# Neighbourhood attention scores as two 128-row matmuls, early loads issued later, and the last token tile normalized on VectorE

## The chip, the cores and the metric

The kernel runs on one core of a Trainium2 chip. The metric is the device time of one execution in microseconds (us), as the median of several runs. All times below are us unless ns is written.

## The reference

A two-layer encoder with model width 1024 runs over two sequences of 256 tokens (512 tokens in all). Layer 0 mixes with neighbourhood attention (8 heads of width 64 over a grid of 4 rows and 64 columns) beside a spatial gating unit; layer 1 mixes with latent attention beside a convolution. Each mixer and each convolutional feed-forward block is followed by a residual sum and a layernorm:

```python
def trunk(x, ...):
    for l in range(DEPTH):                      # DEPTH = 2
        m = even_mixer(...) if l % 2 == 0 else odd_mixer(...)
        x = layernorm(ALPHA * x + m, ln1_g[l], ln1_b[l])
        f = conv_ffn(x, ffn_w_up[l], ffn_conv_w[l], ffn_conv_b[l], ffn_w_down[l])
        x = layernorm(ALPHA * x + f, ln2_g[l], ln2_b[l])
    return x

def even_mixer(x, w_in, rpb, ...):
    h = x @ w_in                                # q, k, v, u, g
    a = neighbourhood_attention(q, k, v, rpb)   # softmax(q k^T / 8 + bias, masked) v
    b = spatial_gating(u, g, ...)
    return jnp.concatenate([a, b], axis=-1) @ w_out
```

## The kernel before

Everything is computed in 32-bit precision out of pairs of rounded numbers: a matrix X is held as hi(X), rounded to the matmul's number format, and lo(X) = X - hi(X). A product of two such matrices is three matmuls (hi hi, hi lo, lo hi). `wload` (L103 to L110) loads 128x1024 weights on SP's DMA queue, ScalarE (ACT) makes the hi part (L107) and VectorE (DVE) the lo part (L109); `split` (L112 to L114) does the same for activations.

The order of the work on each engine is set by a scheduler that simulates the program's timeline (`schedule_with_timeline_sim`, L881); each engine then runs its own list in order and waits on semaphores. `after_mm` (L98) makes an instruction wait for a given matmul: it paces loads.

`even_mixer` (L321) first computes the gating unit's inputs u and g over 8 slices k of the model width: per slice 256 KB of `xT` (tile `xraw`) and 512 KB of weights (`wug`, tile `raw`), both on SP's queue into a ring of four buffers, then 24 matmuls of 512 columns (tiles `u` and `dn`). Other early loads go by GpSimd's (POOL's) queue: parameters `par` (270 KB), the gating unit's layernorm rows `sgr` (512 KB), `sgb` (two of 256 KB), the attention `mask` (32 KB), and sixteen pieces of the attention bias (128 KB each, L388). All of them wait for the matmul `started`, the last of the first four. Fourteen of the sixteen bias pieces are issued ahead of the four small powers `rstd` (L162) of the gating unit's layernorm; POOL then adds the mask to the bias tiles (L392), multiplies and shifts the normalized values `vt` (L377, L378), and makes copies for the scores.

Then come v (`psv`), and, for each of four pairs of heads p, the projections of q (j = 0) and k (j = 1) (24 matmuls each, tile `qk`), written out of PSUM into the operands of the scores. Of the pair's two heads h, head 0 lies in partitions 0 to 63 and head 1 in 64 to 127. `qb` holds for head h hi(q) in the head's own 64 partitions and lo(q) in the other 64; `kh` holds hi(k) for both heads; `kb` holds lo(k) in the head's own partitions and hi(k), copied by POOL (L440), in the other 64. A score block of 128 queries and 256 keys is then

```python
            def score(out, h, qs, ks, qb=qb, kb=kb, kh=kh):
                mm(out, qb[near[h], h, qs], kh[near[h], ks], True, False)
                mm(out, qb[:, h, qs], kb[:, h, ks], False, True)
```

that is, one matmul over 64 partitions (hi hi) and one over 128 (hi lo + lo hi) into the same PSUM columns (tile `s`). There are 32 blocks: four pairs, two sequences, two query halves, two heads. Three sets of `qb` and `kb` serve the four pairs in turn; `kh` comes from another pool.

`attention` (L467) takes scores through DVE (scale and bias `er`, L452; row maximum `nmx`, L478), ACT (exponential, L481), DVE (reciprocal L484, scaling L489), TensorE (PE) transposes (tile `pt`, L494), an ACT copy (`PTr`, L496) and PE again (tile `pv`). Projections of later pairs, the gating unit's matmuls (`sg`) and the first part of the output projection (`op`, `dn`) stand between these in PE's list.

At the end of the kernel `ToOut.done` (L260) normalizes one token tile (128 tokens x 1024) after the other. After the residual sums (L197), the statistics (L258, L263) and POOL's power for the reciprocal deviation (L203), columns 0 to 831 (`ACUT`) are done by DVE in two passes (L268, L276) and leave on SP's queue (L278); columns 832 to 1023 are done by ACT (L271) and POOL (L272, L273) and leave on ACT's queue (L279). For the last tile (t = 3) DVE's second pass is cut in two pieces of 416 columns.

Of the kernel before, what the change touches and what calls it, by code (L numbers as in the profile page):

```python
# [8 lines left out]
F32 = mybir.dt.float32  # L9
F32R = mybir.dt.float32r  # L10
# [5 lines left out]
P = 128  # L16
D = 1024
# [28 lines left out]
def bcast_rows(ap, offset, n):  # L46
    return bass.AP(ap.tensor, offset, [[0, P], [1, n]])
# [3 lines left out]
def tile_encoder(ctx: ExitStack, tc: tile.TileContext, I, O):  # L51
# [23 lines left out]
    def small(w, s="s", tag="small", bufs=24):  # L75
        return sp.tile([P, w], F32, tag=tag, bufs=bufs, name=nm(s))
# [171 lines left out]
    class ToOut:  # L248
# [11 lines left out]
        def done(self, t):  # L260
            x = self.res.x[t]
            mv = small(2, "mv")
            nc.vector.bn_aggr(out=mv, in_=self.st[:, t])  # L263
            r = self.res.rstd(mv[:, 1:2], 1.0)
            a, b = slice(0, ACUT), slice(ACUT, 1024)
            nmr = small(2, "nmr")
            nc.vector.tensor_scalar(out=nmr[:, 0:1], in0=mv[:, 0:1], scalar1=-1.0, scalar2=None, op0=ALU.mult)  # L267
            nc.vector.scalar_tensor_tensor(out=x[:, a], in0=x[:, a], scalar=mv[:, 0:1], in1=self.rows[0][:, a],  # L268
                                           op0=ALU.subtract, op1=ALU.mult)
            nc.gpsimd.tensor_tensor(out=nmr[:, 1:2], in0=nmr[:, 0:1], in1=r, op=ALU.mult)  # L270
            nc.scalar.activation(out=x[:, b], in_=x[:, b], func=AF.Identity, scale=r, bias=nmr[:, 1:2])  # L271
            nc.gpsimd.tensor_tensor(out=x[:, b], in0=x[:, b], in1=self.rows[0][:, b], op=ALU.mult)  # L272
            nc.gpsimd.tensor_tensor(out=x[:, b], in0=x[:, b], in1=self.rows[1][:, b], op=ALU.add)  # L273
            cuts = (0, ACUT // 2, ACUT) if t == NT - 1 else (0, ACUT)
            for c0, c1 in zip(cuts, cuts[1:]):
                nc.vector.scalar_tensor_tensor(out=x[:, c0:c1], in0=x[:, c0:c1], scalar=r,  # L276
                                               in1=self.rows[1][:, c0:c1], op0=ALU.mult, op1=ALU.add)
                nc.sync.dma_start(out=self.y[t][:, c0:c1], in_=x[:, c0:c1])  # L278
            nc.scalar.dma_start(out=self.y[t][:, b], in_=x[:, b])  # L279

    class OutProj:
        def __init__(self, wname, mixT, g0, g1):
# [38 lines left out]
    def even_mixer():  # L321
        xT = []
        psu = [bank(pA, "u") for _ in range(4)]
        psg = dn_banks()
        started = None
        for k in range(KC):
            xr = rawp.tile([P, 1024], F32, tag="raw", name=nm("xraw"))
            x = act([P, 2, T], F32R, "xT")
# [1 line left out]
            if k == 0:  # L330
# [14 lines left out]
                for a, b in ((hi, 0), (hi, 1), (lo, 0)):  # L345
                    for c in range(4):
                        mm(psu[c], a[:, c * P:(c + 1) * P], x[:, b, :], a is hi and b == 0, False)
                    started = started or last_mm[0]
            else:
                nc.sync.dma_start(out=xr[:, :T], in_=I["xT"][k])  # L350
                split(x, xr[:, :T])
# [5 lines left out]
                    mm(psu[c], lo[:, sl], x[:, 0, :], False, k == KC - 1)  # L357
            for t in range(NT):
                gemm_tok([psg[t]], x, t, hi, lo, [slice(512, 1024)], k == 0, k == KC - 1)
        after_mm(nc.gpsimd.dma_start(out=par, in_=I["par"]), started)  # L360
        sgr = act([P, 1024], s="sgr")
        after_mm(nc.gpsimd.dma_start(out=sgr, in_=bcast_rows(I["sgu_rows"], 0, 1024)), started)
        sgb = act([P, 1024], s="sgb")
        after_mm(nc.gpsimd.dma_start(out=sgb[:, :512], in_=bcast_rows(I["sgu_rows"], 1024, 512)), started)
        after_mm(nc.gpsimd.dma_start(out=sgb[:, 512:], in_=I["sgu_wT"]), started)
# [48 lines left out]
        V = [act([P, 2, 512], s="V") for _ in range(2)]  # L414
        for t in range(NT):
            nc.scalar.copy(out=V[t // 2][:, t % 2, :], in_=psv[t])
        qks = [[act([P, 2, T], F32R, s="qk") for _ in range(2)] for _ in range(3)]
        for pair in qks:
            for q_ in pair:
                nc.gpsimd.memset(q_[:, 0, 0:1].bitcast(F32), 0.0)  # L420
        er, PTr = Ring(2, "er"), Ring(2, "PTr")
        for p in range(4):
            bias = biases[p]
            qb, kb = qks[p % 3]
            kh = tmp([P, T], F32R, s="kh")
            near = slice(0, 64), slice(64, 128)
            for j in range(2):
                ps = bank(pA, "qk")
                hi, lo = wload(I["wqk"][:, 2 * p + j].rearrange("p k n -> p (k n)"), 1024)
                gemm_feat(ps, hi, lo, xT)  # L430
                if j == 1:
                    nc.scalar.copy(out=kh, in_=ps)
                for h in range(2):
                    a, b = near[h], near[1 - h]
                    if j == 0:
                        nc.scalar.copy(out=qb[a, h, :], in_=ps[a])
                        nc.vector.tensor_tensor(out=qb[b, h, :], in0=ps[a], in1=qb[a, h, :].bitcast(F32),
                                                op=ALU.subtract)
                    else:
                        nc.gpsimd.tensor_copy(out=kb[b, h, :], in_=kh[a].bitcast(F32))  # L440
                        nc.vector.tensor_tensor(out=kb[a, h, :], in0=ps[a], in1=kh[a].bitcast(F32),
                                                op=ALU.subtract)

            def score(out, h, qs, ks, qb=qb, kb=kb, kh=kh):
                mm(out, qb[near[h], h, qs], kh[near[h], ks], True, False)
                mm(out, qb[:, h, qs], kb[:, h, ks], False, True)
            mixT[p] = act([P, 2, T], F32R, "mixT")

# [437 lines left out]
```

## Time and profile before

| | us |
|---|---|
| median of 3 runs (lowest, highest) | 1129.3 (1129.25, 1130.22) |
| the profiled execution's own time | 1130.04 |
| its span, first to last instruction | 1128.1 |
| PE busy in the span | 1100.6 (98%) |
| DVE busy | 664.6 (59%) |
| ACT busy | 491.0 (44%) |
| POOL busy | 231.6 (21%) |

Busy time of PE is modelled: a matmul is counted from its start to the end of its last column in the array, so consecutive matmuls overlap and a gap between their starts that is longer than usual need not show as idle time. The distance from one matmul's start to the next one's is read off the timeline. The 1.9 us by which the execution is longer than its span lie around the instructions.

### The profile page before, as it was taken

What the parts mean: (1) busy time and instruction counts of PE and PEld (TensorE: products, weight loads), DVE (VectorE), ACT (ScalarE), POOL (GpSimd) and SP (SyncE); (2) the same over time, 40 slices, a digit from 0 to 9 for tenths busy, and PEclk for the clock granted to TensorE, in tenths of its full rate; (3) what the DMA queues carried; (4) which work ended last, traced back from release to release, by engine and by line L of the source; (5) the groups of instructions that cost most, each with busy time, mean ns of one, the idle gap of its engine ahead of it and who ended that gap; (6) DMA issues with size and microseconds to landing.
All of it is one profiled execution on the core that took longest, in us unless ns stands there. A gap on an engine that the chain in (4) does not pass through costs nothing. (4 is left out here: it accounts for less than half of the span.)

```text
span 1128.1 us, 13661 instructions
## 1 busy us (share of the span) xinstructions
PE 1100.6 (98%) x5210; PEld 903.9 (80%) x5210; DVE 664.6 (59%) x996; ACT 491.0 (44%) x785; POOL 231.6 (21%) x231
## 2 busy tenths in 40 slices
PE   9999999999999999999998989999999999999995
PEld 7787767988888888888896767789888888888884
DVE  3567773686656565432369987567656566552226
ACT  3534552554444444321166779545444444431110
POOL 4081001300000000004456743521000000000264
PEclk9999999999999999999999989999999999999998
DMA  9742104343333333645232113135333333222601
GB/s 264 242 121 75 57 20 163 118 134 104 99 94 94 95 102 103 205 132 191 92 114 76 49 54 113 50 100 166 96 94 94 96 101 103 94 94 95 227 15 75
DMA packets 36193, 124.34 MB, mean 110 GB/s; under 512 B 4352, under 2 KB 5120, under 8 KB 36128
## 3 DMA queue, kind: packets, MB, share of 16 engines
q1 hardware_dynamic: 28224, 99.10, 28.8%
q0 software_dynamic: 6480, 22.66, 5.8%
q10 hardware_dynamic: 1424, 1.71, 0.6%
q8 instruction: 41, 0.67, 0.3%
q14 instruction: 24, 0.20, 0.1%
HBM read 114.01 MB, written 8.39 MB: 109 GB/s over the span
## 5 line engine op out<-in xcount | busy, mean ns | idle before, releaser
L96 PE MATMUL up<-xT,whi 128*128 128x512 f32 (+1 forms) x1536 | 440.5, 371 | 0.4 <-DVE xT L245 0.4
L109 DVE TENSOR_TENSOR wlo<-raw,whi 128x1024 fp32r<-128x1024 f32 (+1 forms) x174 | 223.2, 1284 | 303.3 <-ACT whi L107 297.0
L96 PEld LDWEIGHTS up<-xT,whi 128*128 128x128 f32 x1536 | 279.9, 188 | 50.6 <-DVE xT L245 0.6
L107 ACT CAST whi<-raw 128x1024 fp32r<-128x1024 f32 (+1 forms) x174 | 182.5, 1050 | 266.6 <-PE dn L96 132.4
L96 PE MATMUL up<-xT,wlo 128*128 128x512 f32 (+1 forms) x768 | 283.8, 372 | 0.0
L96 PE MATMUL dn<-whi,gT 128*128 128x512 f32 x704 | 217.5, 389 | 0.0
L96 PEld LDWEIGHTS up<-xT,wlo 128*128 128x128 f32 x768 | 144.3, 188 | 25.0
L96 PEld LDWEIGHTS dn<-whi,gT 128*128 128x128 f32 x704 | 132.0, 188 | 27.3
L96 PE MATMUL dn<-wlo,gT 128*128 128x512 f32 x352 | 136.9, 389 | 0.0
L182 POOL DMA_DIRECT2D xres<-xscr x12 | 6.5, 545 | 574.7 <-PE dn L96 573.9
L96 PEld LDWEIGHTS dn<-wlo,gT 128*128 128x128 f32 x352 | 66.1, 188 | 13.7
L113 ACT CAST gT<-cv 128x512 fp32r<-128x512 f32 x44 | 27.3, 620 | 111.9 <-DVE cv L747 111.9
L736 ACT ACTIVATE cv<-up,par 128x512 f32<-128x512 f32 x88 | 68.2, 775 | 0.0
L739 DVE SCALAR_TENSOR_TENSOR cv<-up,par,cv 128x510 f32<-128x510 f32 x88 | 65.7, 747 | 2.7
L737 DVE SCALAR_TENSOR_TENSOR cv<-up,par,cv 128x510 f32<-128x510 f32 x88 | 65.4, 743 | 0.0
L746 ACT ACTIVATE cv<-cv 128x512 f32<-128x512 f32 x44 | 27.8, 632 | 81.9 <-DVE cv L739 81.8
L685 DVE SCALAR_TENSOR_TENSOR cacc<-dpad,par,cacc 128x512 f32<-128x512 f32 x80 | 59.2, 751 | 2.0 <-DVE cacc L685 0.7
L690 POOL TENSOR_TENSOR acc<-acc,pr 128x512 f32<-128x512 f32 x36 | 49.7, 1381 | 35.6 <-ACT pr L689 33.9
L114 DVE TENSOR_TENSOR gT<-cv,gT 128x512 fp32r<-128x512 f32 x44 | 30.4, 691 | 27.5 <-ACT gT L113 27.5
L96 PE MATMUL glu<-xT,khi 128*128 128x512 f32 (+1 forms) x160 | 43.7, 361 | 2.6 <-DVE acc L691 2.6
L96 PE MATMUL dn<-whi,mixT 128*128 128x512 f32 x128 | 42.8, 395 | 0.9 <-DVE mixT L114 0.9
L96 PE MATMUL op<-whi,mixT 128*128 128x512 f32 x128 | 43.6, 399 | 0.0
(194 smaller groups left out, 1372.4 us busy)
## 6 DMA issues: line engine op xcount, KB each, us to landing
raw<-in_wup SPq DMA_DIRECT2D x88, 512.0 KB, 3.6
raw<-in_wdn SPq DMA_DIRECT2D x44, 512.0 KB, 3.5
raw<-in_wout SPq DMA_DIRECT2D x16, 512.0 KB, 3.7
xscr<-xres POOLq DMA_DIRECT2D x12, 512.0 KB, 3.9
xres<-xscr POOLq DMA_DIRECT2D x12, 512.0 KB, 4.7
raw<-in_wqk SPq DMA_DIRECT2D x8, 512.0 KB, 4.7
raw<-in_wglu SPq DMA_DIRECT2D x8, 512.0 KB, 4.0
raw<-in_wug SPq DMA_DIRECT2D x7, 512.0 KB, 5.8
```

Source lines behind the costliest of these rows:

```text
L96: last_mm[0] = nc.tensor.matmul(out=out, lhsT=lhsT, rhs=rhs, start=first, stop=last)
L107: nc.scalar.copy(out=hi[:, :n], in_=raw[:, :n])
L109: nc.vector.tensor_tensor(out=lo[:, :n], in0=raw[:, :n], in1=hi[:, :n].bitcast(F32), op=ALU.subtract)
L113: nc.scalar.copy(out=dst[:, 0, sl], in_=src)
L114: nc.vector.tensor_tensor(out=dst[:, 1, sl], in0=src, in1=dst[:, 0, sl].bitcast(F32), op=ALU.subtract)
L182: after_mm(nc.gpsimd.dma_start(out=x, in_=src[t]), after)
L685: nc.vector.scalar_tensor_tensor(out=a, in0=dpad[i][:, :, j:j + S], scalar=pc("cw", i * 32 + j), in1=a, op0=ALU.mult, op1=ALU.add)
L690: nc.gpsimd.tensor_tensor(out=a2, in0=a2, in1=pr, op=ALU.add)
L736: nc.scalar.activation(out=c, in_=pv, func=AF.Identity, scale=pc(fw, ch * 4 + 1), bias=pc(fw, ch * 4 + 3))
L737: nc.vector.scalar_tensor_tensor(out=c[:, :, 1:S], in0=pv[:, :, 0:S - 1], scalar=pc(fw, ch * 4), in1=c[:, :, 1:S], op0=ALU.mult, op1=ALU.add)
L739: nc.vector.scalar_tensor_tensor(out=c[:, :, 0:S - 1], in0=pv[:, :, 1:S], scalar=pc(fw, ch * 4 + 2), in1=c[:, :, 0:S - 1], op0=ALU.mult, o ...
L746: nc.scalar.activation(out=cg, in_=cg, func=AF.Silu)
```

## The change

It does three things.

1. Scores. hi(k) now goes into a tile `ka` for both halves of the partitions (ACT copies the head's own half, L443 of the changed kernel, POOL copies it to the other half, L444), and `kb` holds lo(k) in the head's own partitions and zeros in the others. Each score block is two matmuls over 128 partitions: `qb` with `ka` and `qb` with `kb`. Instead of one ACT copy of 128x512 per pair there are two of 64x512. The zeros are written once by four POOL memsets of 64x512. Two sets of `qb`, `ka`, `kb` serve the four pairs.
2. Early loads. `sgr` waits for the last matmul of slice k = 3, all the other early loads of POOL's queue for that of slice k = 5.
3. Last token tile. For t = 3 all 1024 columns are normalized by DVE; its second pass is cut into 384, 384 and 256 columns, which leave on SP's, ACT's and SP's queue. ACT and POOL do nothing for this tile but the power.

```diff
--- before.py
+++ after.py
@@ -262,21 +262,24 @@
             mv = small(2, "mv")
             nc.vector.bn_aggr(out=mv, in_=self.st[:, t])
             r = self.res.rstd(mv[:, 1:2], 1.0)
-            a, b = slice(0, ACUT), slice(ACUT, 1024)
-            nmr = small(2, "nmr")
-            nc.vector.tensor_scalar(out=nmr[:, 0:1], in0=mv[:, 0:1], scalar1=-1.0, scalar2=None, op0=ALU.mult)
+            cut = ACUT if t < NT - 1 else D
+            a, b = slice(0, cut), slice(cut, D)
             nc.vector.scalar_tensor_tensor(out=x[:, a], in0=x[:, a], scalar=mv[:, 0:1], in1=self.rows[0][:, a],
                                            op0=ALU.subtract, op1=ALU.mult)
-            nc.gpsimd.tensor_tensor(out=nmr[:, 1:2], in0=nmr[:, 0:1], in1=r, op=ALU.mult)
-            nc.scalar.activation(out=x[:, b], in_=x[:, b], func=AF.Identity, scale=r, bias=nmr[:, 1:2])
-            nc.gpsimd.tensor_tensor(out=x[:, b], in0=x[:, b], in1=self.rows[0][:, b], op=ALU.mult)
-            nc.gpsimd.tensor_tensor(out=x[:, b], in0=x[:, b], in1=self.rows[1][:, b], op=ALU.add)
-            cuts = (0, ACUT // 2, ACUT) if t == NT - 1 else (0, ACUT)
-            for c0, c1 in zip(cuts, cuts[1:]):
+            if t < NT - 1:
+                nmr = small(2, "nmr")
+                nc.vector.tensor_scalar(out=nmr[:, 0:1], in0=mv[:, 0:1], scalar1=-1.0, scalar2=None, op0=ALU.mult)
+                nc.gpsimd.tensor_tensor(out=nmr[:, 1:2], in0=nmr[:, 0:1], in1=r, op=ALU.mult)
+                nc.scalar.activation(out=x[:, b], in_=x[:, b], func=AF.Identity, scale=r, bias=nmr[:, 1:2])
+                nc.gpsimd.tensor_tensor(out=x[:, b], in0=x[:, b], in1=self.rows[0][:, b], op=ALU.mult)
+                nc.gpsimd.tensor_tensor(out=x[:, b], in0=x[:, b], in1=self.rows[1][:, b], op=ALU.add)
+                nc.scalar.dma_start(out=self.y[t][:, b], in_=x[:, b])
+            cuts = (0, 384, 768, D) if t == NT - 1 else (0, ACUT)
+            for i, (c0, c1) in enumerate(zip(cuts, cuts[1:])):
                 nc.vector.scalar_tensor_tensor(out=x[:, c0:c1], in0=x[:, c0:c1], scalar=r,
                                                in1=self.rows[1][:, c0:c1], op0=ALU.mult, op1=ALU.add)
-                nc.sync.dma_start(out=self.y[t][:, c0:c1], in_=x[:, c0:c1])
-            nc.scalar.dma_start(out=self.y[t][:, b], in_=x[:, b])
+                q = nc.scalar if i % 2 else nc.sync
+                q.dma_start(out=self.y[t][:, c0:c1], in_=x[:, c0:c1])
 
     class OutProj:
         def __init__(self, wname, mixT, g0, g1):
@@ -322,7 +325,7 @@
         xT = []
         psu = [bank(pA, "u") for _ in range(4)]
         psg = dn_banks()
-        started = None
+        started = []
         for k in range(KC):
             xr = rawp.tile([P, 1024], F32, tag="raw", name=nm("xraw"))
             x = act([P, 2, T], F32R, "xT")
@@ -345,7 +348,6 @@
                 for a, b in ((hi, 0), (hi, 1), (lo, 0)):
                     for c in range(4):
                         mm(psu[c], a[:, c * P:(c + 1) * P], x[:, b, :], a is hi and b == 0, False)
-                    started = started or last_mm[0]
             else:
                 nc.sync.dma_start(out=xr[:, :T], in_=I["xT"][k])
                 split(x, xr[:, :T])
@@ -357,9 +359,11 @@
                     mm(psu[c], lo[:, sl], x[:, 0, :], False, k == KC - 1)
             for t in range(NT):
                 gemm_tok([psg[t]], x, t, hi, lo, [slice(512, 1024)], k == 0, k == KC - 1)
+            started.append(last_mm[0])
+        early, started = started[3], started[5]
         after_mm(nc.gpsimd.dma_start(out=par, in_=I["par"]), started)
         sgr = act([P, 1024], s="sgr")
-        after_mm(nc.gpsimd.dma_start(out=sgr, in_=bcast_rows(I["sgu_rows"], 0, 1024)), started)
+        after_mm(nc.gpsimd.dma_start(out=sgr, in_=bcast_rows(I["sgu_rows"], 0, 1024)), early)
         sgb = act([P, 1024], s="sgb")
         after_mm(nc.gpsimd.dma_start(out=sgb[:, :512], in_=bcast_rows(I["sgu_rows"], 1024, 512)), started)
         after_mm(nc.gpsimd.dma_start(out=sgb[:, 512:], in_=I["sgu_wT"]), started)
@@ -414,22 +418,21 @@
         V = [act([P, 2, 512], s="V") for _ in range(2)]
         for t in range(NT):
             nc.scalar.copy(out=V[t // 2][:, t % 2, :], in_=psv[t])
-        qks = [[act([P, 2, T], F32R, s="qk") for _ in range(2)] for _ in range(3)]
-        for pair in qks:
-            for q_ in pair:
+        qks = [[act([P, 2, T], F32R, s=s_) for s_ in ("qb", "ka", "kb")] for _ in range(2)]
+        for qb, ka, kb in qks:
+            for q_ in (qb, ka):
                 nc.gpsimd.memset(q_[:, 0, 0:1].bitcast(F32), 0.0)
+            for h in range(2):
+                nc.gpsimd.memset(kb[64 - 64 * h:128 - 64 * h, h, :].bitcast(F32), 0.0)
         er, PTr = Ring(2, "er"), Ring(2, "PTr")
         for p in range(4):
             bias = biases[p]
-            qb, kb = qks[p % 3]
-            kh = tmp([P, T], F32R, s="kh")
+            qb, ka, kb = qks[p % 2]
             near = slice(0, 64), slice(64, 128)
             for j in range(2):
                 ps = bank(pA, "qk")
                 hi, lo = wload(I["wqk"][:, 2 * p + j].rearrange("p k n -> p (k n)"), 1024)
                 gemm_feat(ps, hi, lo, xT)
-                if j == 1:
-                    nc.scalar.copy(out=kh, in_=ps)
                 for h in range(2):
                     a, b = near[h], near[1 - h]
                     if j == 0:
@@ -437,12 +440,13 @@
                         nc.vector.tensor_tensor(out=qb[b, h, :], in0=ps[a], in1=qb[a, h, :].bitcast(F32),
                                                 op=ALU.subtract)
                     else:
-                        nc.gpsimd.tensor_copy(out=kb[b, h, :], in_=kh[a].bitcast(F32))
-                        nc.vector.tensor_tensor(out=kb[a, h, :], in0=ps[a], in1=kh[a].bitcast(F32),
+                        nc.scalar.copy(out=ka[a, h, :], in_=ps[a])
+                        nc.gpsimd.tensor_copy(out=ka[b, h, :], in_=ka[a, h, :].bitcast(F32))
+                        nc.vector.tensor_tensor(out=kb[a, h, :], in0=ps[a], in1=ka[a, h, :].bitcast(F32),
                                                 op=ALU.subtract)
 
-            def score(out, h, qs, ks, qb=qb, kb=kb, kh=kh):
-                mm(out, qb[near[h], h, qs], kh[near[h], ks], True, False)
+            def score(out, h, qs, ks, qb=qb, ka=ka, kb=kb):
+                mm(out, qb[:, h, qs], ka[:, h, ks], True, False)
                 mm(out, qb[:, h, qs], kb[:, h, ks], False, True)
             mixT[p] = act([P, 2, T], F32R, "mixT")
 
```

PE's list is the same but for the stretch from the second pair's projection of k to the first matmuls of the feed-forward block. On PE, the place of the first scores of pair 0 (`qk_814` and `qk_849` are the projections of q and k of pair 1, `s` the scores, `sg` the gating unit) before:

```order
L96 MATMUL qk_814<-xT_370,wlo_819 128x512
L96 MATMUL qk_849<-xT_122,whi_852 128x512 x2
L96 MATMUL s_722<-kh_638,qk_618 128x256
L96 MATMUL qk_849<-xT_122,wlo_854 128x512
L96 MATMUL s_723<-kh_638,qk_618 128x256
L96 MATMUL qk_849<-xT_160,whi_852 128x512
L96 MATMUL sg_711<-sgb_407,vt_411 128x128
```

and now (`qk_997` is the projection of q of pair 2):

```order
L96 MATMUL qk_997<-xT_195,wlo_1002 128x512
L96 MATMUL qk_997<-xT_230,whi_1000 128x512
L96 MATMUL s_724<-ka_619,qb_618 128x256
L96 MATMUL s_724<-kb_620,qb_618 128x256
L96 MATMUL s_724<-ka_619,qb_618 128x256
L96 MATMUL s_724<-kb_620,qb_618 128x256
L96 MATMUL qk_997<-xT_230,whi_1000 128x512
```

The first scores moved back by 32 matmuls of the projections, from the start of pair 1's projection of k into pair 2's projection of q, and the four matmuls of a group now stand together.

On POOL, the early loads before:

```order
masks.py:199 AFFINE_SELECT ident<-ident 128x128
L360 DMA par<-in_par 128x539
L380 DMA mask<-in_mask 128x64
L362 DMA sgr_405<-in_sgu_rows 128x1024
L364 DMA sgb_407<-in_sgu_rows 128x512
L365 DMA sgb_407<-in_sgu_wT 128x512
L388 DMA bias_464<-in_rpb 64x2x256 x4
```

and now:

```order
masks.py:199 AFFINE_SELECT ident<-ident 128x128
L366 DMA sgr_405<-in_sgu_rows 128x1024
L364 DMA par<-in_par 128x539
L368 DMA sgb_407<-in_sgu_rows 128x512
L369 DMA sgb_407<-in_sgu_wT 128x512
L384 DMA mask<-in_mask 128x64
L392 DMA bias_464<-in_rpb 64x2x256 x4
```

`sgr` now leads and `mask` stands behind `sgb`; the loads behind them kept their order.

On POOL, the stretch between the gating unit's values and the first copies for the scores, now (of pair 0 and pair 1):

```order
L424 MEMSET qb_618 128x1
L424 MEMSET ka_619 128x1
L426 MEMSET kb_620 64x512 x2
L424 MEMSET qb_621 128x1
L424 MEMSET ka_622 128x1
L426 MEMSET kb_623 64x512
L396 TENSOR_TENSOR bias_482<-bias_482,mask 128x1024
L426 MEMSET kb_623 64x512
L382 TENSOR_TENSOR vt_411<-vt_411,sgr_405 128x512 x2
L382 TENSOR_TENSOR vt_413<-vt_413,sgr_405 128x512 x2
L444 CAST ka_619<-ka_619 64x512 x2
```

Before, six memsets of 128x1 stood in the place of the eight here, with the same addition and the same shifts of `vt` behind them.

## Rows read from the trace of the kernel before

**Rows 1.** The page, part 4: the chain that ended last, by engine.

```profile
PE 35%; POOL 0%; DVE 0%; POOLq 0%; ACT 0%; issue 0%
```

**Rows 2.** Busy us of PE, PEld, DVE, ACT, POOL by stretch; clock, DMA share, GB/s.

```profile
5.25:50.80 45.55, 44.74 (x192) 35.87 (x193) 20.66 (x22) 19.91 (x24) 11.14 (x19) 1.00 0.92 274
89.40:165.90 76.50, 75.85 (x373) 54.36 (x372) 57.92 (x116) 41.46 (x104) 5.30 (x6) 1.00 0.17 49
100.00:120.00 20.00, 20.00 (x90) 14.40 (x89) 15.94 (x33) 11.01 (x31) 0.99 (x1) 1.00 0.27 79
680.00:690.00 10.00, 10.00 (x63) 7.57 (x59) 9.09 (x21) 9.34 (x29) 0.00 (x0) 0.94 0.00 1
```

**Rows 3.** Timeline of PE, early loads: start, us, instruction, idle before and releaser.

```profile
27.44 0.61 PE L96 MATMUL u<-xT,whi 128*128 128x512 f32 x2
28.34 0.50 PE L96 MATMUL u<-xT,wlo 128*128 128x512 f32 x1 [0.29 <-DVE wlo L109]
...
33.54 0.73 PE L96 MATMUL u<-xT,whi 128*128 128x512 f32 x2
34.80 0.50 PE L96 MATMUL u<-xT,wlo 128*128 128x512 f32 x1 [0.53 <-DVE wlo L109]
```

**Rows 4.** Timeline of PE, one whole group of scores between projections.

```profile
102.39 0.39 PE L96 MATMUL qk<-xT,wlo 128*128 128x512 f32 x1
102.71 0.38 PE L96 MATMUL s<-kh,qk 64*128 64x256 f32 x1
103.02 0.38 PE L96 MATMUL s<-qk,qk 128*128 128x256 f32 x1
...
103.64 0.38 PE L96 MATMUL s<-qk,qk 128*128 128x256 f32 x1
103.86 0.63 PE L96 MATMUL qk<-xT,whi 128*128 128x512 f32 x2
```

**Rows 5.** Timeline of PE, 256-column matmuls over 128 rows in a row.

```profile
205.11 0.40 PE L96 MATMUL up<-xT,whi 128*128 128x256 f32 x2
205.35 0.28 PE L96 MATMUL up<-xT,wlo 128*128 128x256 f32 x1
```

**Rows 6.** Groups of PE by form, from 89.4 to 165.9.

```profile
L96 PE MATMUL s<-kh,qk 64*128 64x256 f32 x32 | 11.4, 381 | 0.0
```

**Rows 7.** Timeline of PE, two 64-row matmuls in a row, then transposes.

```profile
131.80 0.38 PE L96 MATMUL s<-kh,qk 64*128 64x256 f32 x2
```

**Rows 8.** Timeline of POOL's queue from the early loads to the first copies.

```profile
9.65 1.80 POOL L388 DMA_DIRECT2D bias<-in_rpb  x3
...
23.91 0.59 POOL L388 DMA_DIRECT2D bias<-in_rpb  x1 [0.55 <-DMA bias<-in_rpb]
54.22 3.08 POOL L162 TENSOR_TENSOR rstd<-rstd,epsc 128x1 f32<-128x1 f32 x4 [29.72 <-DVE mv L159]
...
73.79 0.27 POOL L420 MEMSET qk<- 128x1 f32 x6
...
77.15 6.02 POOL L378 TENSOR_TENSOR vt<-vt,sgr 128x512 f32<-128x512 f32 x4
85.09 1.78 POOL L440 CAST qk<-kh 64x512 fp32r<-64x512 f32 x2 [1.92 <-ACT kh L432]
```

**Rows 9.** Timeline of all engines, the last token tile.

```profile
1118.56 1.07 DVE L268 SCALAR_TENSOR_TENSOR xres<-xres,mv,rowg 128x832 f32<-128x832 f32 x1
1118.66 1.38 POOL L203 TENSOR_TENSOR v<-v,epsc 128x1 f32<-128x1 f32 x1 [1.73 <-DVE nmr L267]
1120.07 1.24 DVE L276 SCALAR_TENSOR_TENSOR xres<-xres,v,rowb 128x416 f32<-128x416 f32 x2 [0.44 <-POOL v L203]
...
1122.46 0.34 ACTq L279 DMA_DIRECT2D out_y<-xres  x1
```

**Rows 10.** DMA issues: count, KB each, median us from issue to landing.

```profile
out_y<-xres SPq DMA_DIRECT2D x2, 208.0 KB, 1.9
out_y<-xres ACTq DMA_DIRECT2D x4, 96.0 KB, 1.7
```

## The prediction

> **What bounds the kernel now.** I read the chain that ended last first: it is nearly all PE, and of the other engines only the last few microseconds lie on it [rows 1]. So a change counts where it alters the distance between PE's matmuls, or the end behind the last one. Busy time hides such distances, so I then read PE's timeline for starts. Two matmuls of 512 columns last 0.61 together where one lasts 0.39 [rows 3, 4]: starts lie 0.22 to 0.24 apart, 0.227 in long stretches. Matmuls of 256 columns over 128 rows start 0.12 apart, even where each has other weights and adds to the same PSUM columns (three of them from 205.11 to 205.35) [rows 5]. Against these two distances the reader should hold three places: the early loads, the scores, the end.
>
> **The early loads.** From 5.25 to 50.80 PE runs 192 matmuls in 45.55 with the DMA engines 0.92 busy [rows 2]. At 0.227 they take 43.6, so 1.95 are lost. Two places show most of it: the matmul at 28.34 comes 0.45 later than 27.44 plus two distances, and that at 34.80 comes 0.81 late; both wait for a lo part whose weights landed late [rows 3]. In that time POOL's queue issues its 14 bias pieces, from 9.65 to 24.50 [rows 8], through the same DMA engines. After the change none of POOL's loads starts before the end of slice 3, at about 5.25 + 4 x 24 x 0.227 = 27.0, and all but one wait for slice 5, at 37.9, when PE has two of the eight slices left. Gain between 1.0 (if `sgr` and the last two slices still meet) and 1.95; I take 1.8, since every wait seen falls before 37.9.
>
> The moved loads could be late for their readers. If five loads (some 3) and the 14 pieces (14.85 as now) follow from 37.9 on, the queue is free at 55.7, where the powers `rstd` now start at 54.22 [rows 8]: 1.5 late. The new memsets stand behind that on POOL: between 0.045 each (six in 0.27 for 128x1) and 0.89 each (the 64x512 cast, two in 1.78) [rows 8]; four of them are 0.2 to 3.6. POOL would then be ready for the first copies up to 5.1 later. It has 1.9 to spare now (the shifts end at 83.17, the copies start at 85.09 on ACT's word) [rows 8], and the first scores stand 32 matmuls, 7.3, later in PE's list: 9.2 of cover. I cost this at nothing; without cover it would cost those 5.1.
>
> **The scores.** In a whole group the first 64-row matmul starts 0.32 after the projection's (usual 0.227), then each follows 0.31 after the one before it, whichever of the two forms it is, and the projection starts 0.22 after the last (usual 0.12) [rows 4]. Over the usual distances that is 0.09 + 3 x 0.19 + 0.10 = 0.76. The 64-row matmuls have no idle time before them [rows 6], so nothing that they wait for explains it: this is the price of going between 64 and 128 rows. There are 32 64-row matmuls [rows 6], as many of the other form, so 16 groups: 12.2. Some groups are cut up by other work; summed over all 64 starts from 89.43 to 158.72 it is 10.9. The second matmul costs the same before and after. With 128 rows in both, all of it should go. I take 10.9, with 12.2 as the far end.
>
> Against this stands a rule of TensorE: Matmul & The Clock Gate in the Trainium skill, Part 3: Packing small matmuls: matmuls over few rows should be put on different rows of the array, where they run at the same time, and one over few rows alone takes as long as one over all. The trace shows this side by side too: at 131.80 two 64-row matmuls, of the two heads, last 0.38 together, as one does [rows 7]. It happens only twice in 32, because a 128-row matmul stands between nearly all others. By the rule the change would give up 16 pairings of 0.12 each, a loss of 1.9; by the rows it gains 10.9 less those two. I follow the rows, and keep the other as a rival.
>
> Not all of the 10.9 need reach PE's end. From 89.40 to 165.90 DVE is busy 57.92 of 76.50 [rows 2], and its work stays: the same subtractions, from PSUM, of the same size. PE alone would need 65.6, so DVE would have to be busy 0.88 of it. Its densest 20 in this stretch are 15.94, a share of 0.797; in the other layer's attention it reaches 0.909 [rows 2]. At 0.797 its work needs 72.7, a gain of 3.8; at 0.909 it needs 63.7, and PE's 65.6 stand. Neither row is nearer (here the same chain, there a fuller queue), so I take the middle, 0.853: 67.9, a gain of 8.6. ACT gets one more 64x512 cast per pair, with 41.46 busy [rows 2] it has room. That pair 2 now needs pair 0's operand set costs nothing while PE has other work between pair 0's last scores and pair 2's first: 37 projection matmuls, 16 scores and some transposes, about 13, for four casts and four subtractions of at most 0.9 each.
>
> **The end.** POOL's power ends at 1120.04, DVE's first pass at 1119.63 [rows 9]. With 1024 columns in place of 832 the first pass ends near 1119.8, still under the power. Then 832 columns take 1.24 in two pieces [rows 9]; 1024 in three take about 1.24 x 1024/832 + 0.1 = 1.63, so the last DMA issues near 1121.8 instead of 1122.46 on ACT's queue [rows 9]. It carries 128 KB, between the 96 KB that land in 1.7 and the 208 KB in 1.9 [rows 10]. Gain 0.6, between 0.2 and 1.0.
>
> **Sum.** 1.8 + 8.6 + 0.6 = 11.0 off the profiled execution's 1130.04 makes 1119.0. That execution was 0.74 above the median of 1129.3, so the median should be 1118.3. Ends: 1.95 + 12.2 + 1.0 = 15.2 gives 1114.1, 1.0 + 3.8 + 0.2 = 5.0 gives 1124.3.
>
> **Rivals.** (a) DVE sets the pace: PE reaches scores whose PSUM bank DVE hasn't read yet. For it, DVE's share of 0.88; against it, the 18.6 in which it is idle in that stretch [rows 2], of which some must be waiting for the same PE. Gain 3.8 + 1.8 + 0.6: 1123.1. (b) DVE is no limit at all: 10.9 + 1.9 + 0.6 gives 1115.9. (c) Two 64-row matmuls that stand together run at once [rows 7]; the change gives up 16 such pairings of 0.12, and the group's distances have another cause that stays. The scores lose 1.9: 1130.04 - 1.8 - 0.6 + 1.9 is 1129.5, by the median 1128.8, no change. The rule of Part 3 named above would have it so. For it, rows 7; against it, that 30 of the 32 have no partner and the even 0.31 beside 0.12. (d) Slower: the two operand sets. Pair 2's projections can be written out only after pair 0's last scores, pair 3's after pair 1's; if these casts and subtractions stand behind softmax work on ACT and DVE, PE stops at the first scores of pair 2 and of pair 3. It decides from 13 on between pair 0's last scores and the finished operands; to be slower, both stops together must exceed 11. Two of 7 give 1132.3. Against it, DVE's whole share. (e) The change doesn't do what it says: the distance belongs to two matmuls adding to the same PSUM columns, and the moved loads collide with the next weights instead. Then only the end's 0.6 stays, 1128.7; rows 5 speak against the first half.
>
> **Numbers.** Forecast 0.60 (own range 1115.8 to 1121), (a) 0.20, (b) 0.12, (c) 0.03, (d) 0.03, (e) 0.02. The range takes in (a), (b) and the ends: 1115.0 to 1124.0. A measurement of this kernel tells about 0.2% (2.3) from no change. Faster: 0.92; within: (c) and (e), 0.05; slower: (d), 0.03.
>
> **What would show it.** Right: starts 0.12 apart in the score groups and 0.227 around them; no start later than 0.34 between 20 and 36, and 192 matmuls in some 43.8; the last output's DMA issued 1.8 after the power's end instead of 2.4 [rows 9]; the feed-forward block's first matmul some 10 earlier. Wrong: score matmuls of 128 rows still 0.31 apart; PE idle before `s` or `pt` with DVE's `er` as releaser for more than 4 in sum (then (a)), or before `s_1081` with `ka` or `kb` as releaser (then (d)); waits on `raw` between 38 and 60.

## The result and the profile after

The changed kernel takes 1113.44 (median; 1113.30 to 1113.55) against 1129.59 for the kernel before (1129.25 to 1130.22). The ratio is 0.9856, its 95% interval 0.9839 to 0.9873: faster, by about 16, outside the predicted range on the fast side. The profiled executions have spans of 1128.12 and 1111.45, a difference of 16.67. It can be followed along PE's list. Each line of the table below but the last is the start of one matmul that stands in both lists, read off the timeline of PE; the last line is the end of the span.

| | before | after | gained since the line above | predicted |
|---|---|---|---|---|
| v's first matmul | 50.80 | 48.73 | 2.07 | 1.8 |
| feed-forward block: the 4001st matmul from the end | 244.33 | 230.19 | 12.07 | 8.6 |
| last matmul | 1116.30 | 1101.87 | 0.29 | 0 |
| span's end | 1128.12 | 1111.45 | 2.24 | 0.6 |

So the gain of the loads was forecast about right, that of the scores 3.5 too low and that of the end 1.6 too low.

**The loads.** The busy times by stretch of the changed kernel, columns as in [rows 2]; the first stretch runs from the first `u` to v's first matmul, the other two lie in the stage of the scores:

```profile
5.06:48.73 43.67, 43.67 (x193) 36.14 (x194) 20.93 (x23) 21.45 (x28) 7.58 (x13) 1.00 0.84 266
95.50:150.00 54.50, 53.91 (x317) 43.93 (x316) 49.45 (x108) 37.47 (x99) 4.61 (x6) 1.00 0.21 59
100.00:120.00 20.00, 20.00 (x114) 16.79 (x113) 19.39 (x44) 14.88 (x40) 1.28 (x2) 1.00 0.25 71
```

PE has no idle time in the first, where before 0.81 of 45.55 was idle [rows 2]: the same matmuls stand at their usual distance, and between 20 and 36 no start lies more than 0.23 behind the one before it. The weights of the slices now land sooner. The rows give the size and the median from issue to landing, before and after:

```profile
raw<-in_wug SPq DMA_DIRECT2D x7, 512.0 KB, 5.8
raw<-in_wug SPq DMA_DIRECT2D x7, 512.0 KB, 3.5
```

On POOL's queue the loads now come late, and the row that was feared to be late isn't:

```profile
27.44 0.75 POOL L366 DMA_DIRECT2D sgr<-in_sgu_rows  x1 [26.13 <-PE dn L96]
38.32 0.55 POOL L364 DMA_DIRECT2D par<-in_par  x1 [10.13 <-PE dn L96]
...
49.34 3.57 POOL L392 DMA_DIRECT2D bias<-in_rpb  x6 [0.69 <-DMA bias<-in_rpb]
52.92 2.12 POOL L162 TENSOR_TENSOR rstd<-rstd,epsc 128x1 f32<-128x1 f32 x4
...
72.87 1.09 POOL L426 MEMSET kb<- 64x512 f32 x2
...
83.15 1.49 POOL L444 CAST ka<-ka 64x512 fp32r<-64x512 f32 x1
```

The powers `rstd` start at 52.92 (before at 54.22 [rows 8]), one new memset of 64x512 takes some 0.5, and the first copy starts at 83.15 in place of 85.09. PE has no wait on a copy between 66 and 206 (its only stops there are 0.9 in two waits of `pt` for the gating unit, `sgm`). Costing this at nothing was right.

**The scores.** A whole group of the changed kernel on PE's timeline (as [rows 4]), and the two kinds of score matmul over the stage (as [rows 6]: busy time and mean duration in ns):

```profile
97.14 0.39 PE L96 MATMUL qk<-xT,whi 128*128 128x512 f32 x1
97.37 0.28 PE L96 MATMUL s<-ka,qb 128*128 128x256 f32 x1
97.48 0.28 PE L96 MATMUL s<-kb,qb 128*128 128x256 f32 x1
...
97.84 0.40 PE L96 MATMUL qk<-xT,whi 128*128 128x512 f32 x1
```

```profile
L96 PE MATMUL s<-ka,qb 128*128 128x256 f32 x32 | 8.9, 301 | 0.0
L96 PE MATMUL s<-kb,qb 128*128 128x256 f32 x32 | 8.5, 288 | 0.0
```

The starts lie 0.12 apart, the projection follows at 0.12, the first score at 0.23: every excess distance of [rows 4] is gone. Over 95.50 to 150 DVE is busy 0.91 of the time, over 100 to 120 it is 0.97, and PE doesn't wait for it before `s`: DVE keeps up, which the prediction had thought doubtful.

**The end.** The last token tile after the change, all engines:

```profile
1104.07 1.27 DVE L267 SCALAR_TENSOR_TENSOR xres<-xres,mv,rowg 128x1024 f32<-128x1024 f32 x1
1104.23 1.52 POOL L203 TENSOR_TENSOR v<-v,epsc 128x1 f32<-128x1 f32 x1 [1.74 <-DVE v L202]
1105.78 1.54 DVE L279 SCALAR_TENSOR_TENSOR xres<-xres,v,rowb 128x384 f32<-128x384 f32 x3 [0.44 <-POOL v L203]
1106.43 1.26 SPq L282 DMA_DIRECT2D out_y<-xres  x2
1106.96 0.34 ACTq L282 DMA_DIRECT2D out_y<-xres  x1
```

The last output is issued at 1107.36 (the second of SP's two), 1.61 after the power's end at 1105.75; before it was issued 2.42 after it [rows 9]. That is 0.81 less, a little more than the 0.6 that the prediction had. But the span's end came 2.24 closer to PE's last matmul. The end of the chain of waits (start, duration, what), which the prediction passed over, gives the hint. Below stand its last piece before, and from the chain after the piece on the same sequencer and the one behind it:

```profile
1121.80 0.62 POOLq L881
```

```profile
1104.19 1.56 POOLq L885
1105.78 0.62 DVE xres L279
```

POOLq is POOL's sequencer, and L881 and L885 stand for the end of the program: there it waits for POOL to finish. The chain is only a hint: after the change it goes on to DVE's last pass (to 1107.33) and doesn't end on POOL. What came last is read from the trace's own records of the closing wait, before and after:

```
         POOL's last instruction ends   closing wait ends   span ends
before   1122.42 (L273, add)            1127.34             1128.12
after    1105.75 (L203, power)          1110.66             1111.45
```

The closing ends 4.91 behind POOL's last instruction, and the span 0.78 behind the closing, both times; what fills the 4.91 no trace here shows. The last outputs had landed at 1124.15 and 1109.26, some 3.2 and 1.4 ahead of that. The theory to be tested is therefore: (1) the whole price of the scores was the change between 64 and 128 rows, and DVE didn't limit the gain; (2) the end hangs on POOL's last instruction and not on the outputs.

### The profile page after: what moved, and what is told of

Its sections match the earlier page's. It is cut to its first block, busy times and chain, and to the rows that moved or that the text cites. A ratio compares the mean times of both kernels' runs of the same rounds, so it can differ in the third digit from the quotient of the medians.

```text
span 1111.4 us, 13663 instructions
## 1 busy us (share of the span) xinstructions
PE 1087.4 (98%) x5210; PEld 902.1 (81%) x5210; DVE 667.7 (60%) x996; ACT 491.2 (44%) x788; POOL 228.8 (21%) x230
## 5 line engine op out<-in xcount | busy, mean ns | idle before, releaser
L109 DVE TENSOR_TENSOR wlo<-raw,whi 128x1024 fp32r<-128x1024 f32 (+1 forms) x174 | 228.9, 1317 | 290.5 <-ACT whi L107 289.2
L740 ACT ACTIVATE cv<-up,par 128x512 f32<-128x512 f32 x88 | 67.9, 772 | 0.0
L694 POOL TENSOR_TENSOR acc<-acc,pr 128x512 f32<-128x512 f32 x36 | 49.7, 1381 | 35.4 <-ACT pr L693 33.6
```

The source lines that it names most:

```text
L109: nc.vector.tensor_tensor(out=lo[:, :n], in0=raw[:, :n], in1=hi[:, :n].bitcast(F32), op=ALU.subtract)
L694: nc.gpsimd.tensor_tensor(out=a2, in0=a2, in1=pr, op=ALU.add)
L740: nc.scalar.activation(out=c, in_=pv, func=AF.Identity, scale=pc(fw, ch * 4 + 1), bias=pc(fw, ch * 4 + 3))
```

## Experiments

All times in this section that are starts come from PE's timeline of the run in question; "the mark" is the 4001st matmul from the end (244.33 before, 230.19 after). From v's first matmul to the mark the kernel before takes 193.53 and the changed kernel 181.46.

### One part of the change at a time

Edit: the kernel before with the first, the second or the third part of the change's diff, nothing else.

> The kernel before with the change's first part alone (scores as two 128-row matmuls, two operand sets). Theory: the switch between 64 and 128 rows was all that stood between the score matmuls, and DVE does not hold PE back; then the up-projection starts some 12.0 earlier than before and the median is about 1117.5. Rival of the forecast (DVE keeps up a share of 0.853 only): 8.6 earlier, about 1121.0. If the switches were only the 10.9 that the starts add up to: 1118.7. If the full change's 16.2 is a joint effect of the parts, this run falls short of 12 by what only appears together with the others.

> The kernel before with the second part alone (early loads behind slices 3 and 5). Theory: the 24 DMA issues of POOL's queue delayed the lo weights of the gating unit's slices and nothing else; PE's first matmul of v comes 2.1 earlier, the rest keeps its distance, median about 1127.5. Rival: the loads then collide with v's and the projections' weights or delay the powers, and the 2.1 are lost again before the first scores: about 1129.6.

> The kernel before with the third part alone (last token tile on DVE). Theory POOL's end: the end of the execution lies a fixed 5.7 behind POOL's last instruction; that is now the power, 2.4 earlier in the tile than the multiplication and addition were, so the distance from PE's last matmul to the span's end falls from 11.4 to about 9.2 and the median to about 1127.3. Theory of the forecast (the last output's landing sets the end): it falls by 0.6 only, about 1129.0.

| part alone | median | ratio to before, 95% | v's first | v to the mark | last matmul to the span's end |
|---|---|---|---|---|---|
| (before) | 1130.02 | | 50.80 | 193.53 | 11.82 |
| scores | 1118.26 | 0.9897 [0.9884, 0.9911] | 50.84 | 181.43 | 11.82 |
| loads | 1128.46 | 0.9983 [0.9974, 0.9992] | 49.03 | 193.56 | 11.82 |
| end | 1128.33 | 0.9984 [0.9975, 0.9993] | 52.51 | 193.51 | 9.57 |

(The third expectation counts from the end of PE's last matmul, 0.4 behind the start that the table uses. The second speaks of 24 DMA issues; the trace has 19 of POOL's queue before 50.80.) Each part acts in its own place: 12.10, 1.77 and 2.25, in sum 16.1 of the 16.67, so no joint effect is seen. Single executions of the kernel before lie between 1127.83 and 1132.58 on this chip, so that the two small parts are read from the places and not from the medians. The profiled execution of the third part had its v at 52.51, 1.7 late with the loads of before: that stretch is not the same from one execution to the next (50.7 to 52.5 in five executions with the early loads of before, 48.7 to 49.7 in nine with the late ones). The landing of the weights `wug` goes with it: a median of 5.2 to 6.9 in the five and of 3.5 to 3.9 in the nine.

### Row count or order of the list

Edit on the kernel before (PE's order stays but for six matmuls near the first scores):

```diff
-                mm(out, qb[near[h], h, qs], kh[near[h], ks], True, False)
+                mm(out, qb[:, h, qs], kh[:, ks], True, False)
```

and on the changed kernel (here the scheduler made another list for PE, neither that of before nor that of the change):

```diff
-                mm(out, qb[:, h, qs], ka[:, h, ks], True, False)
+                mm(out, qb[near[h], h, qs], ka[near[h], h, ks], True, False)
```

> The kernel before with one edit: the first matmul of each score block reads all 128 partitions of q and of hi(k) instead of the head's 64 (this adds the other head's keys against lo(q), which the reference doesn't have). PE's order stays as before, and nothing moves on DVE, ACT or POOL. Theory: the switch of row counts is the whole price, the scores start 0.12 apart although the groups stand as before: 10.9 to 12.2 faster, 1117.4 to 1118.7. Rival: part of the 12.0 came from the other order of PE's list or from the copies that left the critical place; then this gains clearly less, 6 to 9. Rival: nothing of it is the row count (same PSUM columns): no change.

> The changed kernel with the first matmul of each score block on the head's own 64 partitions only (this leaves out lo(q) times hi(k), which belongs to the reference's product here). All copies, memsets, loads and the end stay. Theory: the price of going between 64 and 128 rows comes back, 0.31 between the starts of a group, 10.9 to 12.2 more, about 1125; the gain is in the row count and not in the new operands. Rival: the gain came from the scores standing together in PE's list, then it costs under 6.

The first: 1119.22, ratio 0.9904 [0.9892, 0.9917]; v to the mark 182.59, 10.94 less. The second: 1124.78, ratio 0.9952 [0.9939, 0.9965]; v to the mark 192.46, 11.0 more than the changed kernel. The score matmuls by form, in the first kernel and then in the second:

```profile
L96 PE MATMUL s<-kh,qk 128*128 128x256 f32 x32 | 8.7, 297 | 0.0
L96 PE MATMUL s<-qk,qk 128*128 128x256 f32 x32 | 8.4, 286 | 0.1
```

```profile
L96 PE MATMUL s<-ka,qb 64*128 64x256 f32 x32 | 11.8, 381 | 0.3 <-DVE er L456 0.3
L96 PE MATMUL s<-kb,qb 128*128 128x256 f32 x32 | 11.6, 367 | 0.0
```

The rows of the first matmul decide: its mean is 297 ns over 128 rows and 381 over 64, and its partner of 128 rows goes with it (286, 367). The 10.94 is the 10.9 that the prediction had from the 64 starts; it is read from the first kernel, where almost nothing else moved, and the second agrees. What the first part of the change gains beyond it, 12.10 - 10.94 = 1.16, came with what else is in that part, the other order of PE's list and the other copies; no run separates the two. Some 0.8 of it lies between the feed-forward block's first matmul and the mark, where one stop is seen. From PE's waits from 66 to 206 in the 128-row kernel with the order of before:

```profile
PE up L96 <- DVE xT L245: 0.4, 1, 0.4
```

The changed kernel doesn't have this stop. The rest was not taken apart.

The first kernel also shows what DVE could do (busy times, columns as in [rows 2]):

```profile
89.40:155.00 65.60, 64.90 (x373) 51.93 (x371) 56.99 (x116) 41.58 (x104) 4.91 (x6) 1.00 0.20 57
```

These are as many matmuls and DVE instructions as stood in the 76.50 of before; DVE is busy 0.87 of the stretch.

### Side by side

The kernel before with the two heads' 64-row matmuls written one behind the other (the 128-row matmuls of a group held back until both are issued, the first 64-row one until DVE has read the last scores, `last_post`):

```diff
-            def score(out, h, qs, ks, qb=qb, kb=kb, kh=kh):
-                mm(out, qb[near[h], h, qs], kh[near[h], ks], True, False)
-                mm(out, qb[:, h, qs], kb[:, h, ks], False, True)
+            def score(outs, qs, ks, qb=qb, kb=kb, kh=kh):
+                for h in range(2):
+                    mm(outs[h], qb[near[h], h, qs], kh[near[h], ks], True, False)
+                    if h == 0 and last_post[0] is not None:
+                        after_mm(last_mm[0], last_post[0])
+                small_mm = last_mm[0]
+                for h in range(2):
+                    mm(outs[h], qb[:, h, qs], kb[:, h, ks], False, True)
+                    tc.add_manual_dep(last_mm[0].ins, small_mm.ins.name,
+                                      mybir.DependencyInfo(mybir.DependencyClass.NoSync, mybir.DependencyReason.DATA),
+                                      reason="pairs")
...
```

> The kernel before with the two heads' 64-row matmuls written side by side, held so by dependencies: of 16 groups 11 then read 64, 64, 128, 128 rows instead of 64, 128, 64, 128. Price by the rows of before: a group then takes 0.32 + 0.003 + 0.31 + 0.12 + 0.12 to 0.22, 0.5 to 0.6 less than now, so 5.5 to 6.6 less over 11 groups, minus what the dependencies make PE wait; about 1124. If the price is per 64-row matmul and not per change between the forms, or another thing of the group, then only the 9 new pairings of 0.12 show: 1.1. If running side by side were as good as 128 rows in both, the up-projection would start 11 to 12 earlier, as with the change's first part.

1128.69, ratio 0.9990 [0.9980, 1.0000]; v to the mark 192.14, only 1.39 less than before. PE's timeline, two groups in a row (x2 is two matmuls merged into one line):

```profile
106.61 0.39 PE L96 MATMUL qk<-xT,whi 128*128 128x512 f32 x1
106.93 0.39 PE L96 MATMUL s<-kh,qk 64*128 64x256 f32 x2
107.24 0.50 PE L96 MATMUL s<-qk,qk 128*128 128x256 f32 x2
107.67 0.39 PE L96 MATMUL s<-kh,qk 64*128 64x256 f32 x2
107.98 0.51 PE L96 MATMUL s<-qk,qk 128*128 128x256 f32 x2
108.33 0.39 PE L96 MATMUL qk<-xT,whi 128*128 128x512 f32 x1
```

Two 64-row matmuls pass in the time of one: their starts are 3 to 4 ns apart. The single starts from the projection at 106.61 on are 106.93, 106.93, 107.24, 107.46, 107.67, 107.67, 107.98, 108.21 and 108.33. So a step into 64 rows from a projection takes 0.32 (usual 0.227), from a score 0.21 (usual 0.12), the step back to 128 rows 0.31, and the step after that still 0.22: going to 64 rows and back costs 0.09 + 0.19 + 0.10 = 0.38, by the pair as much as by the single matmul. Eight scores and the projection ahead of them take 1.72; with the distances of [rows 4] the same nine take 0.32 + 7 x 0.31 + 0.22 = 2.7. The price is thus per change of form, and a pair that stands together saves 0.5 (the 0.38 of one of the two and a step of 0.12). With 128 rows in both, the nine take 0.23 + 8 x 0.12 = 1.2.

The whole list has 11 such pairs, and the kernel before had 2 already, so 9 x 0.5 = 4.5 should have been saved. They didn't arrive, because PE stopped three times (waits from 66 to 206),

```profile
PE op L96 <- DVE qk L441: 1.0, 1, 1.0
PE pt L502 <- ACT PTr L504: 0.7, 1, 0.7
PE s L96 <- DVE er L460: 0.7, 1, 0.7
```

2.4 in all, where the kernel before stops for 0.9 in the same stretch; and around the second of them it lost clock too. The stretch 139 to 147, columns as in [rows 2]:

```profile
139.00:147.00 8.00, 6.28 (x26) 4.10 (x25) 7.32 (x15) 2.55 (x6) 1.22 (x2) 0.79 0.00 1
```

The granted clock is 0.79 there; from 143.60 on the 512-column matmuls start 0.43 apart, the lower of the two levels (1.2 GHz), after PE had been idle 0.7 and 1.0 shortly before. By the distances of its starts the stretch costs some 1.6 beyond the stops; 4.5 - (2.4 - 0.9) - 1.6 = 1.4, and 1.39 was measured. So the price by changes of form is settled, but no kernel here got the pairs without the stops, and PE's list differs from that of before in other places too.

### How much DVE can take

Edit on the changed kernel, in layer 0 for head 0 (8 instructions, shown) or, without `and h == 0`, for both heads (16):

```diff
                 nc.vector.tensor_reduce(out=nmx, in_=sc, axis=AX.X, op=ALU.max, negate=True)
+                if not on_act and h == 0:
+                    again = small(2, "again")
+                    nc.vector.tensor_reduce(out=again, in_=sc, axis=AX.X, op=ALU.max, negate=True)
```

> The changed kernel with DVE's row maximum of head 0 taken a second time in layer 0, into a scratch tile: 8 more instructions of 0.67 on DVE, 5.4 in all, none that PE waits for directly. DVE is busy 55.3 of the 64.7 of the score stretch, 0.855. The forecast's term took a share of about 0.853 for the most that DVE can keep: then the 5.4 all lengthen the stretch, by 5.4/0.853 = 6.3. Theory now: a share seen under PE's pace is no limit; 60.7 of 64.7 is 0.94, still under 1, so PE keeps its pace but for short stops: 0 to 2 longer.

> The same for both heads: 16 more instructions on DVE, 10.7 in all. The forecast's share: 10.7/0.853 = 12.5 longer. Theory now: 66.0 of 64.7 is over 1, so DVE becomes the limit of the stretch; where it has no idle time at all the stretch is 1.3 longer, with DVE's share of 0.97 from the densest 20 it is 3.4 longer, and with some idle at the stretch's ends 3 to 6 longer.

1116.34 with 8 (ratio to before 0.9873 [0.9855, 0.9892]) and 1118.09 with 16 (0.9892 [0.9871, 0.9914]). v to the mark: 184.03 and 186.51, that is 2.6 and 5.1 longer for 5.4 and 10.8 of added work. The stretch 95.50 to 150, with 8 and with 16:

```profile
95.50:150.00 54.50, 52.40 (x306) 42.02 (x305) 52.98 (x110) 36.98 (x94) 5.60 (x6) 1.00 0.20 59
```

```profile
95.50:150.00 54.50, 51.33 (x299) 40.72 (x298) 53.33 (x110) 35.43 (x89) 4.34 (x6) 1.00 0.20 59
```

DVE goes to 0.97 and 0.98 of the stretch, so a share of 0.853 was no limit. But the 2.6 is above the 0 to 2 that I expected, and about half of an added microsecond shows: the changed kernel is probably not far from DVE's limit. This is not shown cleanly, because the scheduler also gave both kernels another order of PE's list. PE's waits from 66 to 206 are 0.9 in the changed kernel, 1.9 with 8 and 4.3 with 16, partly on DVE and partly on ACT; the rest of the 2.6 lies in longer distances between matmuls.

### What sets the end

Two edits on the changed kernel. One adds an instruction that nobody reads behind the last pass, the other takes the last tile's power off POOL:

```diff
+            if t == NT - 1:
+                end = small(2, "end")
+                nc.gpsimd.tensor_tensor(out=end[:, 0:1], in0=x[:, D - 1:D], in1=epsc[:, 2:3], op=ALU.mult)
```

```diff
-        def rstd(self, var, scale):
+        def rstd(self, var, scale, on_act=False):
             v = small(2, "v")
+            if on_act:
+                nc.scalar.activation(out=v[:, 0:1], in_=var, func=AF.Sqrt, bias=epsc[:, 0:1])
+                nc.vector.reciprocal(out=v[:, 1:2], in_=v[:, 0:1])
+                return v[:, 1:2]
...
-            r = self.res.rstd(mv[:, 1:2], 1.0)
+            r = self.res.rstd(mv[:, 1:2], 1.0, t == NT - 1)
```

> The changed kernel with one added instruction: after DVE's last pass over the last token tile, POOL multiplies its last column (128x1) into a scratch tile that nobody reads. Theory POOL's end (the execution ends a fixed 5.7 behind POOL's last instruction): POOL's last instruction moves from 1105.75 to about 1107.5, and the distance from PE's last matmul to the span's end grows by about 1.8, from 9.58 to 11.4, although no output leaves later. Theory of the forecast (the last output's landing sets the end): the outputs land as before, the distance stays at 9.58.

> The changed kernel, for the last token tile the power leaves POOL: ACT takes the square root, DVE the reciprocal. Theory POOL's end: POOL's last instruction is then the addition of the tile before, 3.3 earlier, so POOL no longer sets the end; the distance from PE's last matmul to the span's end falls from 9.58 until the outputs' own end holds it, by 2 to 3, although the outputs leave at most 1.2 earlier. Theory of the forecast: it falls only by as much as the last output lands earlier, 1.2 at most, and by less if ACT has to load a table.

With the added instruction: 1116.33, ratio 0.9878 [0.9866, 0.9891]. POOL's timeline and the chain's last piece:

```profile
1108.47 0.19 POOL L285 TENSOR_TENSOR end<-xres,epsc 128x1 f32<-128x1 f32 x1 [1.66 <-DVE xres L279]
```

```profile
1108.44 0.23 POOLq L888
```

With the power on ACT: 1112.45, ratio 0.9846 [0.9833, 0.9858]. ACT and DVE on the timeline (ACT first loads a table, ACT_TABLE_LOAD):

```profile
1102.51 1.28 ACT L203 ACT_TABLE_LOAD   x1 [1.93 <-POOL xres L279]
1103.81 0.29 ACT L203 ACTIVATE v<-mv,epsc 128x1 f32<-128x1 f32 x1
1104.81 0.16 DVE L204 RECIPROCAL v<-v 128x1 f32<-128x1 f32 x1
1105.01 1.54 DVE L283 SCALAR_TENSOR_TENSOR xres<-xres,v,rowb 128x384 f32<-128x384 f32 x3
```

| from PE's last matmul to | last output issued | POOL's last instruction ends | POOL's closing ends | span's end |
|---|---|---|---|---|
| before | 6.16 | 6.12 | 11.04 | 11.82 |
| changed | 5.49 | 3.88 | 8.79 | 9.58 |
| instruction added | 5.48 | 5.72 | 10.64 | 11.41 |
| power on ACT and DVE | 5.10 | 0.63 | 5.55 | 8.10 |

The instruction of 0.19 lengthens the end by 1.83, although the outputs leave as before. Without the power on POOL the outputs leave 0.39 earlier, and the end comes 1.48 earlier: there POOL's closing is through at 1107.03, SP's closing, which waits for the last output, ends at 1108.82, and the span 0.76 behind it. In all 14 profiled executions of this study POOL's closing ended 4.91 behind POOL's last instruction, and in the 12 of them in which it came last, the span ended 0.78 or 0.79 behind that. In the other two, both with the power on ACT, the outputs set the end.

Once more, both on one chip:

> The changed kernel unaltered, once more beside the next run on the same chip: 1113 to 1115.

> The changed kernel with the last tile's power on ACT and DVE, once more beside the changed kernel on the same chip. Theory POOL's end, as in the first run's rows: 1.5 less than the changed kernel (8.1 from PE's last matmul to the span's end in place of 9.58). If the first run's 1.0 between the medians was chance: no difference.

1113.51 (ratio to before 0.9852 [0.9834, 0.9870]) and 1111.70 (0.9835 [0.9817, 0.9854]); the ends are 9.57 and 8.09 behind PE's last matmul. The second is the fastest kernel of this study: by the rows it beats the changed kernel by 1.5. The two intervals against the kernel before overlap, but its four executions (1110.99 to 1112.64) all lie below the other's four (1113.16 to 1114.48).

## Why the prediction was wrong

- **The early loads**: right. 1.8 predicted, 2.07 and (alone) 1.77 measured; the weights that PE had waited for land in 3.5 in place of 5.8. The cover over POOL's queue held, with the first copy 1.9 earlier and not later. This stretch itself varies by 1.0 to 1.8 from one execution to the next, so that how near the figures come is partly luck.
- **The scores, the price**: right. The 10.9 summed over 64 starts is 10.94 with the order unchanged. Two 64-row matmuls side by side start 3 ns apart. The rule of Part 3: Packing small matmuls (TensorE: Matmul & The Clock Gate, in the Trainium skill) has such matmuls run concurrently, and the trace agrees. What counts here is the change between them and the matmuls around them, 0.38 for going to 64 rows and back, 0.19 for one change in the mean. The Trainium skill says in TensorEngine Tiling (Array Packing), Tiling Modes, Key Properties, "Changing tiling mode (not just tile) drains the TensorE". The traces agree that each change costs, and they give the price; that it is a drain they don't show. Rival (c) counted the pairings alone, and the two kernels of "Row count or order of the list" refute it. (It counts 30 of 32 without a partner; two pairs leave 28. Nothing hangs on it.)
- **The scores, what reaches the end**: this step failed. "Not all of the 10.9 need reach PE's end ... I take the middle, 0.853: 67.9, a gain of 8.6." The 0.797 and the 0.909 were what DVE did while PE set its pace; as ceilings they said nothing. PE got its 65.6: in the 128-row kernel with the order of before the full 10.94 arrive, and DVE does the same 116 instructions, 56.99 busy, in a stretch of 65.6. DVE's ceiling here is not under 0.97, the share that it reached. By that its 57.92 need 59.7 at most, less than PE's 65.6, and the term is the whole 10.9: rival (b) was right on this. The other 1.16 came with the other order and the copies, for which the prediction had no term.
- **The end**: this step failed too. "The last DMA issues near 1121.8 instead of 1122.46" was the right size (the issue moved by 0.67 against PE's last matmul) but the wrong path. Behind the last output there was slack of 3.2; POOL's closing came last. POOL's last instruction ended 6.12 behind the start of PE's last matmul before and 3.88 after, 2.24 less, and the span's end moved by the same 2.24. The row was there: the chain before ended on POOLq, not on SP or ACT.
- The operand sets, rival (d), cost nothing: PE has no wait on `ka` or `kb`. The clock took no part: the two stretches at the lower level between PE's first and last matmul, 6.83 and 13.65 long, are as long after as before.

With 10.9 + 1.16, 2.1 and 2.24 in place of 8.6, 1.8 and 0.6 the sum is 16.4, of the 16.67 measured.

## What to carry to other kernels

Read the price of a matmul off the distance between starts, and count the changes of form in PE's list: two matmuls over 128 rows, half of one operand zeros, in place of one over 64 and one over 128 were worth 11 in 64 matmuls. An engine's share under another's pace is no measure of what it can bear; add work to it, or work out what it needs at nearly full share. At the end, look at which engine's closing comes last, in the records of the closing waits: an engine's last instruction can hold the end for longer than the last output, and the chain does not always show it.

## What the runs showed that was not expected

- POOL's closing: 4.91 behind its last instruction, whatever that was (an addition over 192 columns, a power over one, a multiplication over one).
- The early stretch differs between executions of the same code by up to 1.8 when POOL's loads run beside the weights (50.73 to 52.51), and by 1.0 when they come late (48.73 to 49.68).
- Stops of 0.7 and 1.0 close together were followed by a stretch at the lower level of the clock (0.79 granted over 8), which cost some 1.6 more.
